# Moving loads between the start and the loop, and 16 more matmuls on zeros, in a sparse 3x3 convolution

## Chip, cores, metric

One core of one Trainium2 chip. Times are device microseconds of whole executions; a kernel's time is the median of its runs, slow ones included. A profile is of one execution: the first of a kernel's runs, or, for the kernel before, one run more (127.33 us). Its span is about 1.7 to 1.9 us shorter than the time of the same run. An execution is called slow when it lies over 1.5% above the fastest of its kernel; the ratios use the others alone.

## The reference

```python
batch, c_in, h, w, c_out, k = 16, 64, 64, 64, 128, 3     # float32
# weight: about 90% zeros
x_pad = np.pad(x, ((0, 0), (0, 0), (1, 1), (1, 1)))
output[b, co] += weight[co, ci, kh, kw] * x_pad[b, ci, kh:kh+h, kw:kw+w]   # over ci, kh, kw
```

16.8 MB of input are read and 33.6 MB of output are written. The kernels treat the weight as dense.

## The kernel before

Two images make a pair: 128 partitions of 64 x 64 values. Eight pairs are worked through in order, each in four blocks of 16 rows. GpSimd loads pairs as bf16 (the DMA casts them); SyncE stores the float32 results, one 2 MB transfer for each image. The first 32 rows of pair 0 come from SyncE as float32 and are cast by VectorE and ScalarE.

```python
    nc.sync.dma_start(out=x_head[:, 0:HEAD, :], in_=pair(0)[:, 0:HEAD, :])
    nc.gpsimd.dma_start(out=xs[0][:, HEAD:H, :], in_=pair(0)[:, HEAD:H, :])
    ...
    def load(p):
        nc.gpsimd.dma_start(out=xs[p], in_=pair(p))

    EARLY = 4
    for p in range(1, EARLY):
        load(p)
    ...
    def keep_busy(n):                      # matmuls on zeros: keep TensorE's clock up
        for _ in range(n):
            nc.tensor.matmul(idle_ps, idle_rhs, idle_rhs, start=True, stop=True)

    keep_busy(27)
    # ... weights cast and transposed ...
    keep_busy(12)
    # ... products ...
    for p in range(NP):
        o = [o_pool.tile([C_OUT, H, W], FP32, name="o") for _ in range(2)]
        for blk in range(4):
            ...
                twos(p, o, r0)             # GpSimd adds row pairs, TensorE multiplies, ACT and VectorE evict
                if p > 0 and blk == 1 and p + EARLY - 1 < NP:
                    load(p + EARLY - 1)
            ...
        if not last:
            for n in range(2):
                nc.sync.dma_start(out=out[2 * p + n], in_=o[n])
```

The last pair is stored in four transfers of 1 MB. GpSimd runs up to three blocks ahead of TensorE, so a load that stands in block 1 of pair p is issued while pair p-1 is still being multiplied.

Of the kernel before, what the change touches and what calls it, by code (L numbers as in the profile page):

```python
# [27 lines left out]
def kernel(  # L28
# [6 lines left out]
    nc = tc.nc  # L35

    B, C_IN, H, W = x.shape
    C_OUT, _, KH, KW = weight.shape
    assert (B, C_IN, H, W) == (16, 64, 64, 64) and (C_OUT, KH, KW) == (128, 3, 3)
    NP = B // 2  # L40
# [14 lines left out]
    def pair(p):  # L55
        return x[2 * p : 2 * p + 2].rearrange("n i h w -> (n i) h w")

    xs = [x_pool.tile([128, H, W], BF16, name=f"x{p}") for p in range(NP)]
# [5 lines left out]
    ident = const_pool.tile([128, 128], BF16, name="ident")  # L64
    make_identity(nc, ident)

    def load(p):
        nc.gpsimd.dma_start(out=xs[p], in_=pair(p))  # L68


    EARLY = 4
    for p in range(1, EARLY):
        load(p)


    idle_rhs = const_pool.tile([128, 128], BF16, name="idle_rhs")
# [3 lines left out]
    def keep_busy(n):  # L80
        for _ in range(n):
            nc.tensor.matmul(idle_ps, idle_rhs, idle_rhs, start=True, stop=True)  # L82
# [13 lines left out]
    def cast_x(copy, a, b):  # L96
        copy(out=xs[0][:, a:b, :], in_=x_head[:, a:b, :])  # L97
# [24 lines left out]
    nc.vector.tensor_copy(out=wT[:, G0], in_=ps0)  # L122
    ps2 = transposed(G2)
    nc.scalar.copy(out=wT[:, G2], in_=ps2)
    keep_busy(12)
    cast_x(nc.scalar.copy, 9, 18)
    difference(G01, ps0)
    difference(G21, ps2)
# [26 lines left out]
    def direct(p, o, r0, rows):  # L155
        ps = product(
            [(xs[p], G1, r0, 1), (xs[p], G0, r0 - 1, 1), (xs[p], G2, r0 + 1, 1)], rows
        )
        nc.scalar.copy(out=o[0][:, r0 : r0 + rows, :], in_=ps[0])  # L159
        nc.vector.tensor_copy(out=o[1][:, r0 : r0 + rows, :], in_=ps[1])  # L160

    def twos(p, o, r0):
        t0 = r0 // 2
        s = s_pool.tile([128, 8, W], BF16, name="s")
        nc.gpsimd.tensor_tensor(  # L165
            out=s, in0=xs[p][:, r0 : r0 + 16 : 2, :], in1=xs[p][:, r0 + 1 : r0 + 16 : 2, :], op=ADD
        )
        shared = product([(s, G1, 0, 1)], 8)
        pc = []
        for n in range(2):  # L170
            c = p_pool.tile([128, 8, W], FP32, name="pc")
            nc.scalar.copy(out=c, in_=shared[n])  # L172
            pc.append(c)
        even = [(xs[p], G21, r0 + 1, 2), (xs[p], G0, r0 - 1, 2)]
        odd = [(xs[p], G01, r0, 2), (xs[p], G2, r0 + 2, 2)]
        for first, terms in ((r0, even), (r0 + 1, odd)):
            ps = product(terms, 8)
            for n in range(2):
                nc.vector.tensor_tensor(  # L179
                    out=o[n][:, first : r0 + 16 : 2, :], in0=ps[n], in1=pc[n], op=ADD  # L180
                )

    for p in range(NP):
        o = [o_pool.tile([C_OUT, H, W], FP32, name="o") for _ in range(2)]
        last = p == NP - 1
        for blk in range(4):
            r0 = 16 * blk
            if BLOCKS[p][blk] == "T":
                twos(p, o, r0)


                if p > 0 and blk == 1 and p + EARLY - 1 < NP:
                    load(p + EARLY - 1)
            else:
                for r, rows in ((r0, 8), (r0 + 8, 8)):
                    direct(p, o, r, rows)
            if last and blk % 2 == 1:
                for n in range(2):
                    rows = slice(r0 - 16, r0 + 16)
                    nc.sync.dma_start(out=out[2 * p + n][:, rows, :], in_=o[n][:, rows, :])  # L200
# [3 lines that stand above are left out]
# [30 lines left out]
```

## Time and profile before

| | before |
|---|---|
| time, median of 3 runs (lowest, highest) | 127.21 us (127.09, 127.31) |
| span of the profile | 125.6 us |
| first stores issued | 23.50 us |
| last addition on VectorE ends | 113.66 us |
| DMA share of the sixteen engines, 11 to 121 us | 0.99 to 1.06 in the windows read, of 2 us and more |

In the lines of the profile PE is TensorE, PEld its loading of weights, DVE VectorE, ACT ScalarE, POOL GpSimd and SP SyncE; L146 is line 146 of the kernel; q1 is the DMA queue that SyncE fills, q0 that of GpSimd. In the slices of the page each digit is the busy share of a fortieth of the span, in tenths. A window gives its length, then busy time and number of instructions of PE, PEld, DVE, ACT and POOL. The last three figures are the granted TensorE clock (1 is full speed), the mean busy share of the sixteen DMA engines and the GB/s that were written. A packet counts whole in the window in which it starts, and packets overlap a little in the records, so a share can stand over 1, and the next one then under it. A load counts as its bf16 bytes, half of what is read.

### The profile page before, as it was taken

How to read it: one execution, taken by the hardware profiler on the slowest of the kernel's cores; microseconds unless marked ns; L12 is line 12 of the kernel's file. 1: busy time of each engine (PE TensorE's matmuls, PEld its weight loads, DVE VectorE, ACT ScalarE, POOL GpSimd, SP SyncE). 2: the span in 40 equal slices, each digit the busy share in tenths (PEclk: the TensorE clock that was granted, in tenths of full speed). 3: DMA queues.
4: the chain of work that ended last, by engine and by line, in shares of the span. 5: the costliest groups of instructions: out<-in, count | busy, mean ns of one | idle time of the engine just before them, and what ended most of it. 6: DMA issues, size and time to landing. Idle time of an engine off the chain costs nothing.

```text
span 125.6 us, 2510 instructions
## 1 busy us (share of the span) xinstructions
PE 109.4 (87%) x1014; PEld 56.1 (45%) x1014; DVE 82.3 (66%) x135; ACT 39.0 (31%) x71; POOL 40.6 (32%) x45
## 2 busy tenths in 40 slices
PE   6769999999999999999999999999999999970000
PEld 6624444545454545444554555455545555430000
DVE  0352477877787777888788878877877787772000
ACT  4541533333333333333333333333333333330000
POOL 6327353334433443334333333333333330000000
PEclk9967999999999999999999999999999999999555
DMA  4999999999999999999999999999999999999980
GB/s 119 361 230 214 214 209 219 217 157 399 423 334 305 303 433 311 344 308 407 342 305 329 397 428 444 418 420 423 438 428 444 418 423 423 433 405 423 431 373 26
DMA packets 4044, 42.93 MB, mean 342 GB/s; under 512 B 448, under 2 KB 448, under 8 KB 704
## 3 DMA queue, kind: packets, MB, share of 16 engines
q1 hardware_dynamic: 2880, 34.90, 66.1%
q0 software_dynamic: 1152, 7.86, 30.9%
q8 instruction: 8, 0.13, 0.4%
q14 instruction: 4, 0.03, 0.1%
HBM read 17.07 MB, written 33.55 MB: 403 GB/s over the span
## 4 chain that ended last, share of the span: by engine, by line
PE 83%; DMA 5%; DVE 1%; issue 1%; DVEq 0%; SPq 0%
PE ps L146 83%; DMA o<-in_x_dram 5%; DVE o L179 1%; DVEq L229 0%; DVE x L97 0%; SPq L60 0%; DVEq L179 0%
## 5 line engine op out<-in xcount | busy, mean ns | idle before, releaser
L179 DVE TENSOR_TENSOR o<-ps,pc 128x512 f32<-128x512 f32 x124 | 77.8, 686 | 22.1 <-PE ps L146 19.8
L146 PE MATMUL ps<-x,wT 64*128 64x504 bf16 (+3 forms) x780 | 90.1, 378 | 1.5 <-DVE x L97 1.5
L146 PEld LDWEIGHTS <-wT 64*128 64x128 bf16 x966 | 52.1, 95 | 54.0 <-issue 3.4
L165 POOL TENSOR_TENSOR s<-x 128x512 bf16<-128x512 bf16 x31 | 35.6, 1151 | 59.7 <-PE ps L146 43.3
L172 ACT COPY pc<-ps 128x512 f32<-128x512 f32 x62 | 33.3, 589 | 64.0 <-issue 61.8
L146 PE MATMUL ps<-s,wT 64*128 64x512 bf16 (+1 forms) x186 | 25.5, 377 | 0.0
L82 PE MATMUL ps<-idle_rhs 128*128 128x128 bf16 x39 | 3.9, 283 | 1.0 <-DVE idle_rhs L77 1.0
L82 PEld LDWEIGHTS <-idle_rhs 128*128 128x128 bf16 x39 | 3.5, 133 | 1.0 <-DVE idle_rhs L77 1.0
L68 POOL DMA_DIRECT2D x<-in_x_dram x7 | 3.9, 559 | 0.0
L160 DVE COPY o<-ps 128x512 f32<-128x512 f32 x2 | 1.4, 692 | 3.6 <-PE ps L146 3.6
L101 DVE CAST w_bf<-w_sb 128x192 bf16<-128x192 f32 (+1 forms) x4 | 1.1, 345 | 2.8 <-DMA w_sb<-in_weight_dram 2.8
L159 ACT COPY o<-ps 128x512 f32<-128x512 f32 x2 | 1.2, 586 | 4.0 <-PE ps L146 4.0
L97 ACT CAST x<-o 128x576 bf16<-128x576 f32 (+1 forms) x2 | 1.5, 802 | 1.2 <-DMA o<-in_x_dram 1.2
L97 DVE CAST x<-o 128x576 bf16<-128x576 f32 x1 | 0.5, 460 | 2.0 <-DMA o<-in_x_dram 2.0
L101 ACT ACT_TABLE_LOAD x1 | 1.3, 1283 | 0.7 <-PEq L218 0.7
L101 ACT CAST w_bf<-w_sb 128x64 bf16<-128x64 f32 (+1 forms) x2 | 0.7, 416 | 1.7 <-DMA w_sb<-in_weight_dram 1.7
L107 PE MATMUL ps<-ident,w_bf 128*128 128x128 bf16 x9 | 0.9, 222 | 0.3 <-DVE w_bf L101 0.3
L111 DVE TENSOR_TENSOR wT<-ps,wT 128x384 bf16<-128x384 f32 x2 | 1.0, 550 | 0.0
L63 POOL DMA_DIRECT2D x<-in_x_dram x1 | 0.7, 691 | 0.8 <-POOLq L218 0.8
L107 PEld LDWEIGHTS <-w_bf 128*128 128x128 bf16 x9 | 0.5, 97 | 0.8 <-DVE w_bf L101 0.7
L77 DVE MEMSET idle_rhs<- 128x64 uint32 x1 | 0.1, 112 | 0.8 <-PEq L218 0.8
L122 DVE CAST wT<-ps 128x384 bf16<-128x384 f32 x1 | 0.6, 552 | 0.0
(8 smaller groups left out, 1.9 us busy)
## 6 DMA issues: line engine op xcount, KB each, us to landing
out_dram<-o SPq DMA_DIRECT2D x14, 2048.0 KB, 16.9
x<-in_x_dram POOLq DMA_DIRECT2D x7, 1024.0 KB, 15.5
out_dram<-o SPq DMA_DIRECT2D x4, 1024.0 KB, 10.6
o<-in_x_dram SPq DMA_DIRECT2D x1, 1024.0 KB, 5.7
x<-in_x_dram POOLq DMA_DIRECT2D x1, 512.0 KB, 7.5
w_sb<-in_weight_dram SPq DMA_DIRECT2D x1, 288.0 KB, 3.0
```

The lines of the kernel that those rows point to most:

```text
L68: nc.gpsimd.dma_start(out=xs[p], in_=pair(p))
L82: nc.tensor.matmul(idle_ps, idle_rhs, idle_rhs, start=True, stop=True)
L97: copy(out=xs[0][:, a:b, :], in_=x_head[:, a:b, :])
L101: copy(out=w_bf4[:, g, a:b, :], in_=w_v[:, k : k + b - a, :])
L107: nc.tensor.matmul(wps[:, j, :], src, ident, start=True, stop=True)
L111: nc.vector.tensor_tensor(out=wT[:, g], in0=wps, in1=wT[:, G1], op=SUB)
L146: nc.tensor.matmul(ps[n][:, lo:hi, c_lo:c_hi], tap(g, kw, n), src[q, a:b:step, c_lo + kw - 1 : c_hi + kw - 1], start=(i == 0), stop=(i == ...
L159: nc.scalar.copy(out=o[0][:, r0 : r0 + rows, :], in_=ps[0])
L160: nc.vector.tensor_copy(out=o[1][:, r0 : r0 + rows, :], in_=ps[1])
L165: nc.gpsimd.tensor_tensor(out=s, in0=xs[p][:, r0 : r0 + 16 : 2, :], in1=xs[p][:, r0 + 1 : r0 + 16 : 2, :], op=ADD)
L172: nc.scalar.copy(out=c, in_=shared[n])
L179: nc.vector.tensor_tensor(out=o[n][:, first : r0 + 16 : 2, :], in0=ps[n], in1=pc[n], op=ADD)
```

## The change

More is loaded ahead of the first stores, the other loads come later, and TensorE is to be kept warm until its first product.

```diff
-    def load(p):
-        nc.gpsimd.dma_start(out=xs[p], in_=pair(p))
-    EARLY = 4
+    def load(p, a=0, b=H):
+        nc.gpsimd.dma_start(out=xs[p][:, a:b, :], in_=pair(p)[:, a:b, :])
+    EARLY, CUT = 4, 24
     for p in range(1, EARLY):
         load(p)
+    load(EARLY, 0, CUT)
...
-    keep_busy(12)
+    keep_busy(28)
...
-                if p > 0 and blk == 1 and p + EARLY - 1 < NP:
+                if p == 1 and blk == 3:
+                    load(EARLY, CUT, H)
+                elif p > 1 and blk == 3 and p + EARLY - 1 < NP:
                     load(p + EARLY - 1)
```

## The prediction

> **What bounds the kernel now.** I read the page's slices first, then its DMA lines, then windows over chosen stretches, and the chain of waits last, because that chain can mislead here. The slices, forty of 3.14 us each:
>
> ```profile
> span 125.6 us, 2510 instructions
> ...
> PE   6769999999999999999999999999999999970000
> ...
> DMA  4999999999999999999999999999999999999980
> ...
> q1 hardware_dynamic: 2880, 34.90, 66.1%
> q0 software_dynamic: 1152, 7.86, 30.9%
> ```
>
> TensorE stops four slices before the end, while the DMA engines stand at 9 from the second slice to the last but two. The two queues' packets take 66.1% + 30.9% = 97.0% of sixteen engines' whole span: 121.8 of 125.6 us. So the sixteen DMA engines together are the bound. The windows (us, busy per engine, PE clock, then DMA share and GB/s as the last two figures) show that it holds throughout:
>
> ```profile
> 2.00:7.00 5.00, 3.56 (x41) 3.06 (x39) 1.22 (x5) 1.80 (x6) 2.01 (x5) 1.00 1.00 326
> 7.00:10.50 3.50, 3.07 (x16) 1.31 (x17) 1.77 (x4) 1.43 (x2) 1.99 (x2) 0.54 1.07 221
> 11.00:23.00 12.00, 12.00 (x116) 5.97 (x112) 7.88 (x13) 4.39 (x8) 4.84 (x5) 1.00 1.03 216
> ...
> 25.00:28.00 3.00, 3.00 (x30) 1.49 (x28) 2.27 (x5) 1.07 (x2) 1.15 (x1) 1.00 1.06 156
> 28.00:35.00 7.00, 7.00 (x68) 3.52 (x66) 5.55 (x10) 2.15 (x4) 2.81 (x3) 1.00 0.99 401
> 35.00:45.00 10.00, 10.00 (x98) 5.00 (x95) 7.95 (x14) 3.22 (x6) 3.96 (x4) 1.00 1.02 320
> 75.00:113.00 38.00, 37.30 (x350) 18.48 (x346) 29.71 (x49) 12.48 (x24) 10.06 (x9) 1.00 1.00 426
> 113.00:121.00 8.00, 0.00 (x0) 0.00 (x0) 0.66 (x2) 0.00 (x0) 0.00 (x0) 0.72 1.01 425
> ```
>
> The share stays at 1.00 while the rate moves between 216 and 426. The loads are counted as the bf16 bytes written, half of the float32 bytes read, so a pure load phase at 216 and a pure store phase at 426 are the same load on the engines. Only 25 to 28 us falls below both rates. After 113 us no compute engine has work, and the DMA engines still need until about 124 us.
>
> The chain of waits ends at 113.66 us, with the last addition on VectorE, and puts most of its time on TensorE:
>
> ```profile
> PE 83%; DMA 5%; DVE 1%; issue 1%; DVEq 0%; SPq 0%
> ```
>
> These shares sum to about 90%; the missing tenth is the 12 us of stores after the last instruction. The chain says which computation ended last, not what sets the time. A faster TensorE shortens this chain without moving the DMA end.
>
> **What the Trainium skill says.** "DMA: Bandwidth & Descriptors", section "Issuing engines are not separate DMA queues": transfers from SyncE and GpSimd end on the same sixteen engines and interleave. The same page, "Queues, rings and completion order": an engine takes a whole packet from one queue before it turns to the next. The trace agrees: in the packet records a full load packet (8 KiB written) and a full store packet (16 KiB) both take about 0.62 us, so even sharing would give 16 x 24 KiB in 1.25 us, 315 GB/s; the window 35 to 45 shows 320. "TensorE: Matmul & The Clock Gate", Part 1: the array's clock is halved after an idle window of about 3.4 us, the windows run freely, and a busy one restores it. The trace agrees: the granted clock is 0.54 over 7.0 to 10.5 us, after a pause of TensorE. "Perfetto Trace Analysis", section "What "DMA-bound" means", lists the DMA engines themselves as one of the things that can bind; this is that case.
>
> **The change part by part.**
>
> (a) Sixteen more matmuls on zeros (28 for 12). Here TensorE fell idle just before its first product (start us, us, what):
>
> ```profile
> 5.06 0.83 PE L82 MATMUL ps<-idle_rhs 128*128 128x128 bf16 x12
> 7.43 3.85 PE L146 MATMUL ps<-x,wT 64*128 64x512 bf16 x20 [1.53 <-DVE x L97]
> ```
>
> Twelve took 0.83 us, 69 ns each; 28 take 1.94 us and end at 7.00 us, 0.4 us before the product's operand is ready. So they delay nothing and close 1.1 of the idle 1.53 us. The clock should then stay up. The 36 products of the first direct block took 5.57 us; the later ones run 954 in 103.68 us, 0.109 us each, so 36 would need 3.9 us. TensorE and VectorE finish about 1.6 us earlier, at about 112.0 instead of 113.66, and each pair's stores are issued 1.6 us earlier. On the DMA end this is worth 0: when the last stores of the kernel are issued in 113 to 114 us, the engines have a queue, shown by the share of 1.01 all the way to 121 us. In bytes: 8 us at 425 GB/s plus the rest (116 GB/s over the last 4.6 us) is 3.9 MB after 113 us, while the last two stores hold 2.1 MB. Some 1.8 MB, about 4 us, stood ahead of them.
>
> (b) 24 of pair 4's 64 rows move up front, and the other 40 and pairs 5 to 7 are issued two blocks later. No bytes are added or removed. GpSimd issued the four late loads at 18.16, 30.96, 43.77 and 56.58 us; two blocks are about 6.4 us (12.81 between loads, four blocks), so 24.6, 37.4, 50.2 and 63.0, minus up to 1.6 for the faster start. Cost: one pair's load is cut in two. In the packet records 4 KiB took 0.324 us and 8 KiB 0.624, which leaves 0.024 fixed per packet; each engine gets eight packets more, 8 x 0.024 = 0.2 us, plus 0.02 for one more completion. Total +0.2 us.
>
> (c) Does the DMA ever run dry? Before, three pairs (about 4.9 us each in the landings) were through at 23 to 24 us and load 4 filled until 29. After, the up-front part ends 24/64 x 4.9 = 1.8 us later, at about 25. The first stores were issued at 23.50; with (a) 21.9. They hold 4.2 MB, 9.8 us at 426 GB/s, and the rest of pair 4 is 3.1 us: work until about 38. Pair 1's stores, before at 36.25, come at 34.7. So a queue of some 3 us stands there, and 1.5 us even without (a). Then each pair brings 9.8 + 4.9 = 14.7 us of DMA work in 12.8 us of computation, so the queue grows. Gaps: 0.
>
> (d) Can a late load stall the computation? Load 7, issued at about 63 us, should land within 20 us (the slowest landing before was 20.6), by 83. GpSimd wants pair 7 about three blocks before TensorE gets there at 7.43 + 7 x 13 = 98, so at 88. About 5 us to spare, and no stall. Loads 5 and 6 have as much or more.
>
> (e) The dip at 25 to 28 us. A pure load phase would move 3 x 213 = 640 GB/s.us and a mix more; 156 x 3 = 468 passed: about 0.8 us lost. In the packet records the load packets there last up to 1.3 us, from about 2 us after the first stores' issue until the stores' first packet, 4.4 us after issue. With the loads ending near 25 this overlap is shorter: perhaps -0.4 us.
>
> The sum is +0.2 - 0.4 + 0 = -0.2, within my uncertainty of nothing. I chose 127.1 against 127.21 before.
>
> **The rivals.**
> 1. TensorE sets the end, as the chain suggests: 127.2 - 1.6 = 125.6. For it speaks only the chain; against it the 12 us of stores after the last addition. Even this is under 2%.
> 2. The change from loads to stores opens a hole. The first store's data took 4.4 us from issue to its first packet. Were that a fixed delay, the stores would start at 21.9 + 4.4 = 26.3 while loads end at 25: 1.3 us idle, 128.5. Against it: the first weight load began about 1.3 us after its issue on idle engines, and late loads that join busy engines also took about 4 us. That looks like a queue to get through, which empties with the loads.
> 3. The clock still drops, or the extra matmuls run at the slow rate (27 took 3.03 us at the start, 112 ns each; 28 would take 3.1 us and end at 8.2, 0.7 us too late). Then pair 1's stores come at 36 to 37 us, with the queue nearly empty: 127.2 to 127.8.
> 4. A late load stalls GpSimd and with it TensorE. It must exceed 5 us to bite, and then the 12 us between compute end and DMA end absorb much: at most about 128.
>
> **Range and chances.** Centre 127.1. Rival 1 or a larger gain from the dip gives the low side, 126.2; rivals 2 and 3 the high side, 128.3. The three runs before span 0.22 us, so noise is small. Faster by over 2% needs under 124.7, which means removing 2.5 us from a DMA that is idle for almost none of its 122 us: 3%. Slower by over 2% needs over 129.75, two rivals together: 4%. Within 2%: 93%.
>
> **What would show it right or wrong.** (a) right: granted clock 1.0 over 7 to 10.5 us, last addition near 112, and a span that does not follow. (b) the two halves of pair 4 as separate issues, the others near 36 to 37, 49 and 62 us. (c) the DMA share at 1.0 from 2 to 121 us; a window under 0.9 near 25 or 37 us would prove rival 2 or 3. (d) no wait of GpSimd on a load. (e) more than 156 GB/s in the window where loads give way to stores. I am wrong if the time falls by as much as TensorE's gain, or if a DMA gap of over 1 us appears.

## The result

| | before | changed |
|---|---|---|
| time, median of 4 runs (lowest, highest) | 127.15 us (127.02, 127.31) | 126.53 us (126.46, 126.82) |
| span of the profile | 125.6 us | 124.7 us |
| first stores issued | 23.50 us | 21.83 us |
| last addition on VectorE ends | 113.66 us | 111.98 us |

The ratio is 0.9955, with a 95% interval of 0.9935 to 0.9975. A ratio here is the mean time of one kernel's fast runs over that of the other's in the same rounds, so it is not quite the ratio of the medians. The change is a gain of about half a per cent: small, but clear of the noise.

The changed kernel's page, the lines that answer to those of before:

```profile
span 124.7 us, 2543 instructions
...
PE   6999999999999999999999999999999999940000
...
PEclk9999999999999999999999999999999999998555
DMA  4999999999999999999999999999999999999991
...
q1 hardware_dynamic: 2880, 34.90, 66.6%
q0 software_dynamic: 1296, 7.86, 30.8%
```

The DMA is still at 9 throughout. The software queue has 1296 records instead of 1152: 128 more data packets and one more completion on each of sixteen engines, for the same 7.86 MB.

Its windows:

```profile
7.00:10.50 3.50, 3.21 (x32) 1.75 (x32) 2.38 (x5) 1.93 (x3) 2.07 (x2) 1.00 1.10 227
11.00:23.00 12.00, 12.00 (x116) 6.36 (x114) 8.27 (x14) 4.88 (x9) 5.42 (x6) 1.00 1.02 212
23.00:25.00 2.00, 2.00 (x22) 1.01 (x18) 2.00 (x4) 0.15 (x1) 0.51 (x2) 1.00 1.13 222
25.00:28.00 3.00, 3.00 (x31) 1.58 (x28) 2.27 (x4) 0.92 (x2) 1.09 (x1) 1.00 1.04 416
28.00:35.00 7.00, 7.00 (x70) 3.70 (x66) 5.55 (x10) 2.65 (x6) 2.71 (x3) 1.00 1.01 330
...
75.00:113.00 38.00, 35.62 (x334) 18.56 (x330) 29.28 (x47) 11.82 (x22) 9.22 (x8) 1.00 1.00 426
113.00:121.00 8.00, 0.00 (x0) 0.00 (x0) 0.00 (x0) 0.00 (x0) 0.00 (x0) 0.59 1.00 422
121.00:125.00 4.00, 0.00 (x0) 0.00 (x0) 0.00 (x0) 0.00 (x0) 0.00 (x0) 0.50 0.19 82
```

Two things differ. The granted clock over 7 to 10.5 us is 1.00 instead of 0.54. And the window 25 to 28 us, which moved 156 GB/s before, under the rate of pure loads and of pure stores, now moves 416. The pure phases run at the old rates, 212 and 426.

TensorE's start (start us, us, what, idle time before and what ended it), then the end of the chain of waits:

```profile
5.33 1.73 PE L84 MATMUL ps<-idle_rhs 128*128 128x128 bf16 x28
7.35 3.99 PE L148 MATMUL ps<-x,wT 64*128 64x512 bf16 x36 [0.29 <-DVE x L99]
```

```profile
111.38 0.60 DVE o L181
```

L148 and L181 are the lines that were L146 and L179 before. The 36 products of the first block take 3.99 us instead of 5.57. Every computation afterwards is some 1.6 us earlier, yet the span is only about 0.8 us shorter. Whether the one gave the other is what the experiments must tell.

How long the changed kernel's split load takes (issuing engine and operation, number, KB, median us to landing):

```profile
x<-in_x_dram POOLq DMA_DIRECT2D x1, 640.0 KB, 14.0
...
x<-in_x_dram POOLq DMA_DIRECT2D x1, 384.0 KB, 24.6
```

The 24.6 us are from an issue at 4.1 us, behind four other loads: most of it is time in the queue.

**A measure for what follows.** Each DMA packet stands in the trace with its size and time. A packet of one kind nearly always takes the same time: 0.62 us for 8 KiB written by a load, 0.61 for 16 KiB of a store. Around the change from loads to stores some take up to 1.3 us. I call "stretch" the sum of the time over the usual of all data packets that start between 20 and 46 us and are over by more than 0.03 us, divided by sixteen engines. Before it is 1.20 us (loads 1.14, stores 0.06), in the changed kernel 0.52 us (loads 0.44, stores 0.08). It is from one profile of each kernel.

### The profile page after: what moved, and what is told of

Read it like the earlier page. It is cut to its first block, busy times and chain, and to the rows that moved or that the text cites. A ratio compares the mean times of both kernels' runs of the same rounds, so it can differ in the third digit from the quotient of the medians.

```text
span 124.7 us, 2543 instructions
## 1 busy us (share of the span) xinstructions
PE 109.0 (87%) x1030; PEld 59.5 (48%) x1030; DVE 82.3 (66%) x135; ACT 39.0 (31%) x71; POOL 41.1 (33%) x46
## 3 DMA queue, kind: packets, MB, share of 16 engines
q0 software_dynamic: 1296, 7.86, 30.8%
## 4 chain that ended last, share of the span: by engine, by line
PE 82%; DMA 5%; DVE 1%; issue 1%; DVEq 0%; SPq 0%
PE ps L148 82%; DMA o<-in_x_dram 5%; DVE o L181 1%; DVEq L233 0%; DVE x L99 0%; SPq L60 0%; DVEq L181 0%
## 5 line engine op out<-in xcount | busy, mean ns | idle before, releaser
L181 DVE TENSOR_TENSOR o<-ps,pc 128x512 f32<-128x512 f32 x124 | 77.8, 686 | 22.1 <-PE ps L148 19.8
L148 PE MATMUL ps<-x,wT 64*128 64x504 bf16 (+3 forms) x780 | 88.7, 373 | 0.3 <-DVE x L99 0.3
L148 PEld LDWEIGHTS <-wT 64*128 64x128 bf16 x966 | 54.4, 94 | 48.9 <-issue 0.3
L148 PE MATMUL ps<-s,wT 64*128 64x512 bf16 (+1 forms) x186 | 25.7, 377 | 0.0
L84 PE MATMUL ps<-idle_rhs 128*128 128x128 bf16 x55 | 4.8, 265 | 1.0 <-DVE idle_rhs L79 1.0
L84 PEld LDWEIGHTS <-idle_rhs 128*128 128x128 bf16 x55 | 4.4, 123 | 1.0 <-DVE idle_rhs L79 1.0
L68 POOL DMA_DIRECT2D x<-in_x_dram x8 | 4.4, 561 | 0.0
L63 POOL DMA_DIRECT2D x<-in_x_dram x1 | 0.7, 693 | 0.8 <-POOLq L222 0.8
L122 ACT CAST wT<-ps 128x384 bf16<-128x384 f32 x1 | 0.5, 480 | 0.4 <-PE ps L109 0.4
## 6 DMA issues: line engine op xcount, KB each, us to landing
x<-in_x_dram POOLq DMA_DIRECT2D x1, 384.0 KB, 24.6
```

What stands on the lines that cost most here:

```text
L68: nc.gpsimd.dma_start(out=xs[p][:, a:b, :], in_=pair(p)[:, a:b, :])
L148: nc.tensor.matmul(ps[n][:, lo:hi, c_lo:c_hi], tap(g, kw, n), src[q, a:b:step, c_lo + kw - 1 : c_hi + kw - 1], start=(i == 0), stop=(i == ...
L181: nc.vector.tensor_tensor(out=o[n][:, first : r0 + 16 : 2, :], in0=ps[n], in1=pc[n], op=ADD)
```

## The experiments

Theory A: the gain comes from the DMA alone. When the first stores start while a long queue of loads is in the engines, the running packets are stretched for some us; with the loads ahead of them nearly finished, less is stretched. Theory B: the gain comes from the computation, which starts faster. Theory C: the first store has a fixed delay, so a hole opens if the loads end too early. Theory D: the gain comes from the later issue of pairs 5 to 7. Theory E: the stretch is a cost of the very first store. A1 and A2 are variants of A, told where they are tested. All runs were correct, and all timed runs shared their rounds with the kernel before, whose medians in the three sessions, on three chips, were 127.18, 127.09 and 127.18 us.

### e1: the matmuls alone

```diff
 # the kernel before
-    keep_busy(12)
+    keep_busy(28)
```

> The kernel before with 28 instead of 12 matmuls on zeros, loads untouched. Theory A (the gain of 0.6 us comes from loads no longer coexisting with the start of the first stores): TensorE ends about 1.6 us earlier, the first stores are issued at about 21.9 us, pair 4's load still holds the engines until about 29 us, load packets there are still stretched to over 1 us, and the time stays at 127.1 (ratio 0.999 to 1.002). Theory B (the earlier computation gives the gain): 126.5 (ratio 0.995).

Measured: 127.06 us, ratio 0.9999 (0.9987 to 1.0012). Its windows at the change from loads to stores:

```profile
23.00:25.00 2.00, 2.00 (x22) 0.93 (x20) 1.76 (x3) 0.07 (x1) 0.25 (x1) 1.00 1.26 201
25.00:28.00 3.00, 3.00 (x32) 1.34 (x30) 2.27 (x5) 1.07 (x2) 1.16 (x1) 1.00 0.86 254
```

The clock stayed at 1.00 over 7 to 10.5 us, the first stores were issued at 22.14 us, the last addition ended 1.4 us earlier (112.29), and the time did not move. B falls. The stretch is 0.80 us: the stores still start into a long queue of loads, 1.4 us earlier than before.

### e2 and e12: the loads alone

```diff
 # the changed kernel
-    keep_busy(28)
+    keep_busy(12)
```

> The changed kernel with 12 instead of 28 matmuls on zeros, so only the loads move. Theory A: the first stores are issued at about 23.5 us, the loads up front end at about 25, the overlap is short, few stretched packets, and the time is that of the changed kernel or a little less, 126.3 to 126.6 (ratio 0.993 to 0.996). Theory B: 127.1 or, with the split's cost, 127.3 (ratio 1.000 to 1.002).

Measured: four fast runs of 126.42 to 126.81 us, ratio 0.9962 (0.9947 to 0.9977); two more were slow (129.05 and 130.28). The profile fell on a slow one, where the first product began only at 9.48 us, so I draw nothing on the time from it. It shows one thing that the others don't: the first stores were issued at 25.49 us, and the DMA share fell to 0.82 over 23 to 25 us and to 0.67 over 25 to 28. With the computation that late, the shortened loads left a hole. The kernel was run once more for a fast profile.

> The changed kernel with 12 matmuls on zeros once more, because the profile of the first such run fell on a slow execution. Expected in a fast one: granted clock near 0.5 for some us after 7 us, last addition about 1.6 us later than in the changed kernel, first stores issued near 23.5 us, DMA share 1.0 or a small hole between 25 and 26 us, and the time 126.4 to 126.8 (ratio 0.994 to 0.997).

Measured: 126.39 us, ratio 0.9933 (0.9911 to 0.9956). So the loads give the whole gain without the extra matmuls, and A holds. Stretch: 0.43 us. But my expectation of the clock failed. The start of TensorE in this profile:

```profile
5.23 0.92 PE L84 MATMUL ps<-idle_rhs 128*128 128x128 bf16 x12
7.28 3.99 PE L148 MATMUL ps<-x,wT 64*128 64x512 bf16 x36 [1.13 <-DVE x L99]
```

With 12 matmuls and 1.13 us of idle TensorE the clock did not drop here: 36 products took the same 3.99 us, the first stores were issued at 21.76 us. The 5.57 us of the profile before were thus not the sure effect of 12 matmuls; they are what one execution had. Of the five profiles with 12 matmuls three show a drop (before, e8 and the slow one of e2), of the nine with 28 none: few, but the extra matmuls may well make it rarer. As the computation was as early here as in the changed kernel, no fast profile shows what the loads are worth when the clock does drop.

### e3, e6, e10, e7, e4: how many rows up front

Each is the changed kernel with another cut; the rest of pair 4 is issued where the 40 rows were, and the pieces of 0 rows are left out.

```diff
-    EARLY, CUT = 4, 24
+    EARLY, CUT = 4, 0      # e3; e6: 12; e10: 18; e7: 40; e4: 64
```

> The changed kernel with no rows of pair 4 up front: its whole load is issued where the 40 rows are now. Loads up front end at about 23 us, the first stores are issued at 21.9. Theory A with no fixed delay of the first store: no stretched packets, no split to pay, so 126.1 to 126.4 (ratio 0.992 to 0.994). Theory C (the first store needs a delay of about 3 us from issue to first packet whatever the engines do): a hole of 1 to 2 us in the DMA share between 23 and 26 us, 127.3 to 128.3 (ratio 1.002 to 1.009).

> The changed kernel with 12 rows of pair 4 up front instead of 24. Loads up front end near 23.9 us, the first stores are issued at 22. Theory A1 (the cost arises only in the first overlap, and ends with the loads up front): few stretched packets, 126.3 to 126.6 (ratio 0.992 to 0.996). Theory A2 (there is one start-up cost for the first time that loads and stores truly mix; if the first overlap is too short for it, it comes back when the rest of pair 4 joins the stores, as in the run with no rows up front): stretched store packets between 26 and 30 us and 127.0 (ratio 0.998 to 1.001).

> The changed kernel with 18 rows of pair 4 up front, between the two cuts that were fast (12 and 24). Theory A: little stretch on either side, 126.4 to 126.5 (ratio 0.994 to 0.995). It would also be the best version seen if it falls under the 126.45 of 12 rows.

> The changed kernel with 40 rows of pair 4 up front instead of 24. Loads up front end near 26.1 us, when the first stores, issued at 22.2, have their first packet. Both A1 and A2: the overlap is whole, some 20 to 30 stretched packets, so the gain is gone or mostly gone: 126.9 to 127.2 (ratio 0.998 to 1.000). If the gain came from cutting the load at all or from its later part being late: 126.5 (ratio 0.995).

> The changed kernel with all 64 rows of pair 4 up front in one load, nothing of it later. Loads up front end at about 28 us, the first stores are issued at 21.9. Theory A: the overlap is back, with some 40 to 60 stretched load packets, and the time is near the kernel before: 127.0 to 127.4 (ratio 0.999 to 1.002), although no split is paid. Theory D (the gain comes from the later issue of pairs 5 to 7, which this keeps): 126.3 to 126.5 (ratio 0.993 to 0.995).

| rows up front | time, us | ratio (95%) | stretch of loads + stores, us |
|---|---|---|---|
| 0 (e3) | 127.05 | 0.9996 (0.9982 to 1.0009) | 0.01 + 1.02 |
| 12 (e6) | 126.45 | 0.9982 (0.9941 to 1.0024) | 0.02 + 0.36 |
| 18 (e10) | 126.53 | 0.9944 (0.9923 to 0.9964) | 0.09 + 0.32 |
| 24 (the change) | 126.53 | 0.9955 (0.9935 to 0.9975) | 0.44 + 0.08 |
| 40 (e7) | 127.34 | 1.0017 (0.9998 to 1.0036) | 1.01 + 0.04 |
| 64 (e4) | 127.06 | 1.0000 (0.9988 to 1.0013) | 0.81 + 0.06 |

The ratio of 12 rows is blurred by two of its six runs, 127.51 and 128.13 us, that count as fast; the other four lie between 126.41 and 126.47. I found no cause for the two. e10 had one slow run of 131.36.

The gain has a window: 18 and 24 rows have it, 12 in four runs of six; 0, 40 and 64 have not. D falls with e4, which issues pairs 5 to 7 as late as the changed kernel does and gains nothing. My expectation for e3 missed on both sides. There was no hole: its first store was issued at 22.06 us and had its first packet 0.85 us later, with a DMA share of 1.00 in the window 23 to 25, so C falls. (By the times that packets ran, about 0.2 us of the engines' time between 22 and 23 us was idle, not the 1 to 2 us of C.) And there was no gain either, because the stretch moved. The windows of e3:

```profile
23.00:25.00 2.00, 2.00 (x22) 0.88 (x18) 1.84 (x4) 0.00 (x0) 0.69 (x2) 1.00 1.00 406
25.00:28.00 3.00, 3.00 (x32) 1.37 (x28) 2.27 (x5) 1.07 (x2) 1.14 (x1) 1.00 0.90 355
28.00:31.00 3.00, 3.00 (x32) 1.37 (x28) 2.27 (x5) 1.07 (x2) 1.15 (x1) 1.00 1.03 268
```

The stores run alone at 406 GB/s, then pair 4's whole load joins them: 26 store packets that start between 26 and 30 us take over 0.7 us. With 12 rows 15 store packets do, but not at the full cost. So neither A1 (no cost after the first overlap) nor A2 (the whole cost comes back) is quite right: with 12 to 24 rows about 0.4 to 0.5 us is paid, in one place or shared between the two; outside it is 0.9 to 1.1.

### e9 and e11: when the rest of pair 4 follows

```diff
 # the changed kernel
-                if p == 1 and blk == 3:
+                if p == 1 and blk == 1:      # e9; e11: p == 2 and blk == 1
                     load(EARLY, CUT, H)
```

> The changed kernel, but the other 40 rows of pair 4 are issued two blocks earlier, at about 16.6 us, where the kernel before issued the whole pair. Same packets, same cuts, same later loads as in the changed kernel; only now the loads run on without a pause through the first stores' start-up. If the gain comes from having no loads left when the stores start (theory A): it is gone, stretched load packets near 24 to 26 us, 127.1 to 127.3 (ratio 1.000 to 1.002). If it comes from the cut as such or from the later pairs' issue: 126.5 (ratio 0.995).

> The changed kernel with the other 40 rows of pair 4 issued two blocks later, near 29 us. If the moment at which the rest joins the stores does not matter once the first overlap was short: 126.4 to 126.6 (ratio 0.994 to 0.996). If joining later costs a stretch of the store packets, as in the run with no rows up front: stretched store packets near 31 to 34 us and 126.9 to 127.2 (ratio 0.998 to 1.000). It stalls nothing: GpSimd wants these rows near 52 us.

Measured: e9 127.46 us, ratio 1.0014 (0.9992 to 1.0036); e11 126.55 us, ratio 0.9943 (0.9920 to 0.9966); each had one slow run more. Stretch 1.20 us in e9, 0.49 in e11. The windows of e9:

```profile
23.00:25.00 2.00, 2.00 (x22) 1.04 (x19) 1.64 (x3) 0.19 (x1) 0.37 (x1) 1.00 1.05 137
25.00:28.00 3.00, 3.00 (x30) 1.60 (x28) 2.27 (x5) 1.07 (x2) 1.16 (x1) 1.00 1.04 235
```

e9 is the sharpest test. It has the changed kernel's packets, cuts, matmuls and later loads; only the issue of the 40 rows is two blocks earlier, so that loads are still queued when the stores start. The window 23 to 25 us falls to 137 GB/s, and the gain is gone. e11 shows that a later issue costs nothing.

### e5: the cut by itself

```diff
 # the kernel before
-                    load(p + EARLY - 1)
+                    if p == 2:
+                        load(5, 0, 24)
+                        load(5, 24, H)
+                    else:
+                        load(p + EARLY - 1)
```

> The kernel before with pair 5's load cut into 24 and 40 rows, both issued at its old place, far from the change from loads to stores. The sum of the prediction: +0.2 us (ratio 1.0015) from eight more packets on each engine at 0.024 us each and one more completion. If a split costs nothing: ratio 1.000. The packet records should show the 3 KiB and 5 KiB packets at 0.25 and 0.40 us, 0.65 together against 0.624.

Measured: 127.11 us, ratio 1.0000 (0.9985 to 1.0014). The packets are as expected, 0.247 and 0.398 us, together 0.021 over the uncut 0.624; eight of them make 0.17 us on each engine. The time doesn't show it. The interval's upper end is 0.18 us, so the expected cost is at its very edge: inconclusive, but not more than that.

### e8: a small store first

```diff
 # the kernel before, after the memset of the zeros for TensorE
+    zeros = const_pool.tile([128, 2, W], FP32, name="zeros")
+    nc.vector.memset(zeros, 0.0)
+    nc.sync.dma_start(out=out[B - 1][:, H - 2 : H, :], in_=zeros)
```

> The kernel before with one small store of zeros (512 bytes per partition) to two rows of the output issued right after the head's load; the rows are written again later with their right values. Theory E (the stretch is a cost of the first store or the first touch of the output at all): it moves to the early store, where it is short, and the load packets near 25 to 28 us stay at 0.62 us: 126.3 to 126.6 (ratio 0.993 to 0.996). If it is a cost of a long stream of stores joining a queue of loads: stretched packets near 25 to 28 us as before, 127.2 to 127.4 (ratio 1.000 to 1.002).

Measured: 127.05 to 128.56 us in five fast runs and one slow, ratio 1.0048 (1.0010 to 1.0087). E falls: no run gained anything. The profile, of a run of 128.32 us, still has 1.67 us of stretch, so its size isn't to be compared with the others, but the stretch did not leave. Why these runs scatter is open.

### Together

Stretch against time sorts the kernels of the table, e1, e5, e9, e11 and e12 into two groups with nothing between: 0.38 to 0.52 us of stretch with 126.39 to 126.55 us, and 0.77 to 1.20 us with 127.05 to 127.46; before and the changed kernel are one of each. Within a group the order is not kept. The middle of the groups' ranges differs by 0.53 us in stretch and by 0.79 in time. The last store's landings, one on each of the sixteen engines, show where the difference comes from. Their mean is 122.04 to 122.18 us in the first group and 122.41 to 122.89 in the second, 0.54 apart in the middle, as the stretch is. The last of the sixteen, for which the kernel waits, is 123.43 to 123.59 and 124.13 to 124.41, 0.76 apart, as the time is. So the time that an engine loses to stretched packets is not made good before the end, and the engine that ends last lags a little further behind the mean in the second group; why it does is open.

No version beats the changed kernel clearly. e12, without the extra matmuls, has the lowest median, 126.39 us; its interval overlaps that of the change.

## Why the prediction was right

The time of 126.53 lies within the range, near its low side, the class (within 2%) was right, and the mechanism of the gain was named, as part (e). The size was not: the sum of -0.2 was called nothing, and the time fell by 0.6 us, clear of the noise. By its steps:

- **The bound.** Right. The DMA share stayed at 1.0 to 121 us, and computation that ended 1.4 us earlier bought nothing by itself (e1).
- **(a)** Right in the numbers: 28 matmuls ended at 7.06 us (7.00 predicted, though 62 ns each and not 69), the last addition at 111.98 (112.0). Wrong in two inferences. That they "delay nothing" is not sure: in e1 the same 28 took 2.46 us and held the first product until 7.64, 0.2 us after its operand was cast. And 12 matmuls don't always lead to a drop of the clock: e12 and e5 had 12 and kept it. Nor does the trace agree with the cited page as fully as I wrote: TensorE's pause before the drop was 1.53 us, less than half of the 3.4 us named there, and e5 kept the clock over a pause of 1.35. What agrees is that the clock is halved, for 3.41 us (7.28 to 10.69), and comes back.
- **(b)** The late loads were issued at 35.69, 48.49 and 61.30 us, as predicted. The cost of +0.2 us was not seen: 0.17 by the packets, at most 0.18 by the time (e5).
- **(c)** Right: no window read between 11 and 121 us has a DMA share under 1.00.
- **(d)** Right: the list of waits of the changed kernel has none of GpSimd on a load.
- **(e)** The term that was mis-sized. I estimated -0.4 us of a loss of 0.8; the measured time fell by 0.6. In the two profiles the stretch fell from 1.20 to 0.52, so by 0.7. One profile doesn't fix that: e1 and e5, with the loads of before up front and no gain, show 0.80 and 0.77, so the fall may be as small as 0.3.
- **Rival 1** fell with e1, **rival 2** with e3. In the changed kernel the first store's packet came 2.9 us after its issue, in e3 0.85: the less is queued, the sooner (0.85, 1.5, 1.9 and 2.9 us with 0, 12, 18 and 24 rows up front, then 4.4 and 4.2 with 40 and 64). **Rival 3** is absent from the changed kernel, whose clock stayed at 1.00; **rival 4** fell with (d). Two figures of rival 2 were read roughly: the packet records give 4.2 us before (not 4.4) and 1.0 us for the weights' load (not 1.3). Nothing hangs on it.

The sum of -0.2 missed the -0.6 through (e), which gave more, and through as much of (b)'s +0.2 as was not paid. That the time still fell within the range owes something to the range, which was wide (126.2 to 128.3) against a change of 0.6.

## What to carry to other kernels

When the DMA engines are full from end to end, shifting work on a compute engine moves only the chain of waits; look for windows where their rate falls under that of either pure phase although their share is 1. Here such a window stands where the first stores meet queued loads, and the cheap remedy was to end the loads about when the first stores start, then issue the rest. Test a combined change by its halves: one half here did everything, and the other looked as if it had.

## What the Trainium skill lacked or had wrong

- "DMA: Bandwidth & Descriptors", "Queues, rings and completion order", gives the taking of turns between queues but no cost of the moment when a second kind of transfer joins a full queue. These runs: packets of up to 1.3 us instead of 0.62, 0.4 to 1.2 us per engine in all. Why it happens, why later loads that join the stores mostly don't cause it, and why a short first overlap makes it smaller stays open.
- The same page, "Where 436 GB/s comes from", says that the HBM side binds at about 358 GB/s for transfers between HBM and SBUF. With one core in use the stores ran at 426 GB/s for 38 us. Read alone, the sentence misleads: that about 358 is each core's part when two stream at once stands only further up, in the note to the page's measured table.
- The same page, "Latency and other measured facts", gives 0.6 us to the first byte for transfers issued from SyncE. Counted from the end of the issuing instruction, the weights' load (0.64 us) and the first store of e3 (0.50 us) agree. With loads queued ahead the first store took 2.6 us (the changed kernel) and 3.9 us (before); that table has no such case.
